# A hybrid decoder layer on one core: doubling steps of a triangular inverse on packed odd rows, and rows of norms by transposes of a repeated column

## The chip, the cores and the metric

The program runs on one core of a Trainium2 chip. The metric is device time in microseconds, as a median of runs. The five engines have a queue each: TensorE (PE in the profile; PEld are its weight loads), VectorE (DVE), ScalarE (ACT), GpSimd (POOL) and SyncE (SP), which issues the DMAs.

## The reference

One decoder layer for a prompt of 2048 tokens (width 1024) and for 8 single-token samples: a mixer, a cross-attention into 256 memory tokens, a SwiGLU, each behind an RMS norm and added to the residual. The mixer's two halves read one input projection: a convolution of width 31, and a gated DeltaNet with 4 heads of 128, whose chunked form solves a unit lower triangular system per chunk and head:

```python
def rms_norm(x, g, eps=1e-6):
    xf = x.astype(jnp.float32)
    y = xf * lax.rsqrt(jnp.mean(xf * xf, axis=-1, keepdims=True) + eps)
    return (y * g.astype(jnp.float32)).astype(x.dtype)
...
    decay = jnp.exp(jnp.where(incl, gc[..., :, None] - gc[..., None, :], -jnp.inf))
    kb = k * beta[..., None]
    lower = jnp.where(strict, jnp.einsum('nbhid,nbhjd->nbhij', kb, k) * decay, 0.0)
    a_mat = lower + jnp.eye(c, dtype=lower.dtype)
    u = lax.linalg.triangular_solve(a_mat, v * beta[..., None], left_side=True, lower=True, unit_diagonal=True)
    w = lax.linalg.triangular_solve(a_mat, kb * jnp.exp(gc)[..., None], left_side=True, lower=True,
                                    unit_diagonal=True)
```

## The kernel before

Activations lie with channels on partitions and tokens along the free axis, in 4 blocks of 512 tokens (b = 0 to 3). The large products split their operands into a high and a low fp32r part and make three passes of them. They run in this order: the input projection for the blocks 0 and 1, then 2 and 3 (tiles hd, glua, glub); the memory's keys and values and the products folded from them (mkv, wk, vp); output projection and attention of the blocks 0 and 1 (rg, sc, rg); then per block the FFN (fx, fy, fz, dn), with output projection and attention of block 2 behind the first FFN and of block 3 behind the second. The first FFN also makes sums of weights that the later ones read back.

Beside these run lanes, Python generators that yield what they wait for. One lane per block and head, `dn_front`, builds the inverse T of the triangular matrix for its 4 chunks of 128 tokens (16 fronts in all); `dn_chain` then runs the recurrence over the chunks. The convolution's taps are 30 VectorE instructions per 128 channels and block (tile cacc).

A front stores lt, the transposed lower matrix, in DRAM and reads its 16x16 diagonal blocks back into 32 partitions, where `base_inverse` inverts them on VectorE (tiles w, x, bit, biq). It writes the inverse blocks to zw and their transposes to zt, both zero elsewhere, and reads W and Tm from there, as 4 chunks of 128x128. Three doubling steps follow, for blocks of s = 16, 32 and 64 (`LEV`). Each makes a product pu1 of lt and Tm, masks and negates it into u1 on VectorE, makes a product pu2 of W and u1, and adds it into Tm's left columns on VectorE; four transposes (ptw) and a ScalarE copy give the next W. The last step only makes the corner block of W, with products of 64 columns. `u1` is one constant tile, 128 x 4 x 128, zeroed at the start. All these products are plain fp32.

A norm's row vector is needed on all partitions. `rstd` gives the reciprocal root r with tokens on partitions (128 x 4, or 128 x 2 for half a block). `spread` turns it: VectorE multiplies the identity by r into dg (128 x 512), TensorE multiplies dg by a matrix of ones (fp32, tile prs), and ScalarE copies the bank to rsb. It runs 13 times: for the input norm of the four blocks, the FFN norm of the four, the final norm of three, and twice, 256 columns each, for the last block's final norm, whose second is on the last stretch of the program.

No instruction goes to an engine as it is written: all are recorded, and `Tape.order` lists them by its own costs and latencies, ready times, free buffers and PSUM banks. Each engine then runs its list in order. There are 8 PSUM banks: 3 "mm" for the large products, 3 "s" for the lanes' steps, one "o" for the chain's output and one "cv" for the convolution; the large products may use the last two only when no chain or no convolution is open. Since every operation is issued by the recorder, all have the line L469 in the profile, and groups are told apart by their tiles; the tiles pu1 and pu2 stand there as pu, and u1 as u. Names of buffers that come from one pool tile (kd, vn, rb and at of a front are halves of tiles named dn) are those of the tile.

Of the kernel before, what the change touches and what calls it, by code (L numbers as in the profile page):

```python
# [14 lines left out]
P = 128  # L15
# [576 lines left out]
def hybrid_step(ctx: ExitStack, tc: tile.TileContext, i: dict, o: list):  # L592
# [486 lines left out]
    def spread(r, n, both=False, spare=RES):  # L1079

        nt = n // P
        yield ("t2", 2 + spare)
        dg = t2("dg", (P, nt, P))
        rb_ = t2("rsb")[:, :n]
        V.tensor_tensor(out=dg, in0=bc(ident, 1, [P, nt, P]), in1=bc(r, 2, [P, nt, P]), op=ALU.mult)
        yield dg
        yield ("ps", "s")
        pb = ps("prs", shape=(P, n))
        mm(pb, ones, dg.rearrange("p t j -> p (t j)"), True, True)
        drop(dg)  # L1090
        A.activation(out=rb_, in_=pb, func=AF.Copy)
        if both:
            return pb, rb_
        yield rb_
        return rb_
# [497 lines left out]

    def base_inverse(x, w, tmp_):
# [4 lines left out]
        for s in (2, 4, 8):  # L1599
# [8 lines left out]
            for step in range(2):  # L1608
# [17 lines left out]
                yield ("dve", 1500)  # L1626

    def dn_front(h, b, sc, prev, out):
# [90 lines left out]
        dma(z_diag(zw[z]), w16[:, 0:256].rearrange("p (j i) -> p j i", i=16))  # L1719
        dma(z_diag(zt_[z]), t16.rearrange("p (j i) -> p j i", i=16))  # L1720
        drop(bit, du)
        W = t2("W", (P, NT, P))
        dma(W, z_full(zw[z]))
# [7 lines left out]
        def left(x, s):  # L1731
            return x.rearrange("p c (b e s) -> p c b e s", e=2, s=s)[:, :, :, 0, :]

        for s in LEV:
            yield ("ps", "s")
            pu = ps("pu1", shape=(P, NT, P))
            for c in range(NT):
                mm(pu[:, c, :], lt[:, c, :], Tm[:, c, :], True, True)
            msk = bc(nms[s].rearrange("p (b s) -> p b s", s=s), 1, [P, NT, 64 // s, s])
            V.tensor_tensor(out=left(u1, s), in0=left(pu, s), in1=msk, op=ALU.mult)  # L1740
            yield u1
            yield ("ps", "s")
            pu = ps("pu2", shape=(P, NT, P))
            if s == LEV[-1]:

                for c in range(NT):
                    mm(pu[0:64, c, 64:P], u1[:, c, 0:64], W[:, c, 64:P], True, True)
                V.tensor_copy(out=W[0:64, :, 64:P], in_=pu[0:64, :, 64:P])
                break
            for c in range(NT):  # L1750
                mm(pu[:, c, :], W[:, c, :], u1[:, c, :], True, True)
            V.tensor_tensor(out=left(Tm, s), in0=left(pu, s), in1=left(Tm, s), op=ALU.add)
            yield Tm
            yield ("ps", "s")
            pt = ps("ptw", shape=(P, NT, P))
            for c in range(NT):
                transpose(pt[:, c, :], Tm[:, c, :], ident)
            drop(W)
            W = t2("W", (P, NT, P))
            A.activation(out=W, in_=pt, func=AF.Copy)  # L1760
            yield W
        drop(lt, Tm)
# [151 lines left out]
    for s in LEV:  # L1914
        m = const(f"nms{s}", [P, 64])
        GS.memset(m, -1.0)
        nb = 64 // s
        GS.affine_select(out=m, in_=m, compare_op=ALU.is_ge, fill=0.0, base=-s, pattern=[[-2 * s, nb], [0, s]], channel_multiplier=1)
        GS.affine_select(out=m, in_=m, compare_op=ALU.is_ge, fill=0.0, base=2 * s - 1, pattern=[[2 * s, nb], [0, s]], channel_multiplier=-1)
        nms[s] = m  # L1920
# [30 lines left out]
    zw = [dram.tile([32, 2064], F32, tag=f"zw{k}", name=f"zw{k}") for k in range(NZ)]  # L1951
# [6 lines left out]
    for k in range(NZ):  # L1958
        for z in (zw[k], zt_[k]):
            dma(z.rearrange("a b -> (a b)").rearrange("(p x) -> p x", p=P), zt)  # L1960
    drop(zt)

    u1s = [const("u1", [P, NT, P])]
    GS.memset(u1s[0], 0.0)
# [879 lines left out]
```

## Time and profile before

| | |
|---|---|
| median of 3 runs | 3009.05 us (3008.03 to 3018.47) |
| the profiled execution | 3007.98 us, span 3006.1 us |
| mean granted TensorE clock | 0.994 |
| busy | PE 2935.5, PEld 2610.7, DVE 2082.1, ACT 1303.0, POOL 1405.4 us |
| instructions of the profile | 53090 |

A matmul of the recorder in fp32 is two MATMUL records in the profile, one in fp32r or a transpose is one. The end of a matmul is modelled, and matmuls overlap their neighbours, so a group's price is better read from starts than from durations. The lists of an engine's instructions, further down, show order alone; they have no times.

### The profile page before, as it was taken

To read this page: it belongs to the slowest core of one execution; us is meant where nothing else is said; L and a number is where in the kernel's file an instruction comes from. 1 tells how busy PE (TensorE), PEld (TensorE's weight loads), DVE (VectorE), ACT (ScalarE), POOL (GpSimd) and SP (SyncE) were. 2 spreads that over 40 slices of the span, in tenths; PEclk is the share of its full clock that TensorE was granted. 3 is DMA by queue.
4 is the path that set the end of the run, shared out by engine and by line. 5 is a ranking of instruction groups with operands and counts; after the bars stand their busy time and mean duration, and the time that the engine had idled before them with its cause. 6 is when DMAs were issued, how large, how long until landed. Compare 5 with 4: busy or idle time off the path is not lost.

```text
span 3006.1 us, 53090 instructions
## 1 busy us (share of the span) xinstructions
PE 2935.5 (98%) x18950; PEld 2610.7 (87%) x18950; DVE 2082.1 (69%) x4280; ACT 1303.0 (43%) x2651; POOL 1405.4 (47%) x1245
## 2 busy tenths in 40 slices
PE   9999999999999999979999999999999999999998
PEld 7899978888888888879988779988888999999997
DVE  8868999988659775987688974543766444664345
ACT  6533455343564434535544453433454233333233
POOL 4434343333645555767886114445413344344444
PEclk9999999999999999999999999999999999999999
DMA  6443334544693433557777657877625666676673
GB/s 218 153 123 95 123 109 135 169 128 131 213 298 106 132 97 93 202 193 265 250 246 268 228 183 238 262 229 228 197 88 170 216 222 216 212 239 218 222 221 129
DMA packets 355175, 560.95 MB, mean 187 GB/s; under 512 B 56448, under 2 KB 154688, under 8 KB 354896
## 3 DMA queue, kind: packets, MB, share of 16 engines
q1 hardware_dynamic: 354912, 557.57, 57.6%
q8 instruction: 150, 2.46, 0.3%
q14 instruction: 113, 0.93, 0.1%
HBM read 449.38 MB, written 108.64 MB: 186 GB/s over the span
## 4 chain that ended last, share of the span: by engine, by line
PE 82%; DVE 10%; DMA 4%; issue 2%; ACT 1%; POOL 1%; SPq 0%; DVEq 0%; POOLq 0%; ACTq 0%
PE dn L469 16%; PE fy L469 12%; PE rg L469 10%; PE hd L469 9%; PE fx L469 8%; PE fz L469 8%; PE sc L469 5%; DVE cacc L469 3%; PE pu L469 2%; PE glua L469 2%; PE glub L469 2%; DVE bit L469 1%; PE pch L469 1%; DVE acc L469 1%; DMA w<-sums 1%
## 5 line engine op out<-in xcount | busy, mean ns | idle before, releaser
L469 POOL TENSOR_TENSOR w<-raw,w 128x512 fp32r<-128x512 f32 x689 | 937.9, 1372 | 965.3 <-ACT w L469 919.0
L469 ACT ACTIVATE w<-raw 128x512 fp32r<-128x512 f32 x912 | 567.7, 630 | 846.7 <-PE fx L469 174.6
L469 PE MATMUL dn<-ff,w 128*128 128x512 f32 (+2 forms) x2688 | 513.5, 347 | 1.2 <-DVE ffs L469 0.5
L469 PEld LDWEIGHTS dn<-ff,w 128*128 128x128 f32 x2688 | 422.8, 188 | 63.2 <-DVE ff L469 1.0
L469 PE MATMUL fy<-op,w 128*128 128x256 f32 (+1 forms) x3168 | 426.2, 282 | 6.9 <-DVE w L469 2.8
L469 PE MATMUL hd<-hT,w 128*128 128x512 f32 (+2 forms) x1920 | 406.7, 360 | 6.2 <-ACT w L469 6.2
L469 PEld LDWEIGHTS fy<-op,w 128*128 128x128 f32 x3168 | 398.7, 189 | 13.7 <-DVE w L469 3.7
L469 DVE SCALAR_TENSOR_TENSOR cacc<-cu,cw,cacc 128x512 f32<-128x512 f32 x480 | 358.0, 746 | 11.5 <-ACT cacc L469 6.9
L469 PEld LDWEIGHTS hd<-hT,w 128*128 128x128 f32 x1920 | 305.6, 191 | 49.6 <-ACT w L469 7.0
L469 DVE TENSOR_TENSOR x<-dn,x 128x512 f32<-128x512 f32 (+1 forms) x448 | 254.0, 571 | 131.1 <-PE dn L469 128.1
L469 PE MATMUL fx<-op,w 128*128 128x256 f32 (+1 forms) x2112 | 285.7, 283 | 11.1 <-ACT ffu L469 11.0
L469 PE MATMUL fz<-op,w 128*128 128x256 f32 (+1 forms) x2112 | 287.7, 283 | 1.8 <-DMA w<-sums 1.7
L469 PEld LDWEIGHTS fx<-op,w 128*128 128x128 f32 x2112 | 269.2, 190 | 18.5 <-ACT ffu L469 11.5
L469 PEld LDWEIGHTS fz<-op,w 128*128 128x128 f32 x2112 | 266.5, 189 | 5.7 <-issue 4.2
L469 DVE TENSOR_TENSOR w<-raw,w 128x512 fp32r<-128x512 f32 x223 | 196.1, 886 | 66.8 <-ACT w L469 66.1
L469 POOL TENSOR_TENSOR sqj<-sqj,sqj 128x512 f32<-128x512 f32 (+1 forms) x98 | 135.0, 1377 | 214.0 <-ACT sqj L469 209.5
L469 DVE TENSOR_TENSOR ffu<-fy,ffu 128x256 f32<-128x256 f32 (+1 forms) x176 | 74.4, 423 | 176.8 <-PE fy L469 176.6
L469 PE MATMUL rg<-catS,w 128*128 128x512 f32 (+1 forms) x960 | 192.1, 354 | 0.8 <-DVE x L469 0.8
L469 PE MATMUL rg<-pT,w 128*128 128x512 f32 x768 | 192.4, 399 | 0.2 <-ACT pT L469 0.2
L469 PE MATMUL sc<-w,hT 128*128 128x512 f32 x768 | 188.5, 399 | 3.3 <-DVE x L469 1.7
L469 PEld LDWEIGHTS rg<-catS,w 128*128 128x128 f32 x960 | 152.0, 188 | 24.2 <-DVE x L469 1.2
L469 PEld LDWEIGHTS sc<-w,hT 128*128 128x128 f32 x768 | 141.2, 188 | 35.9 <-ACT pr L469 3.2
(376 smaller groups left out, 4120.1 us busy)
## 6 DMA issues: line engine op xcount, KB each, us to landing
w<-sums SPq DMA_DIRECT2D x264, 512.0 KB, 4.4
raw<-in_w_gate_dram SPq DMA_DIRECT2D x176, 256.0 KB, 3.1
sums<-w SPq DMA_DIRECT2D x88, 512.0 KB, 3.9
raw<-in_w_down_dram SPq DMA_DIRECT2D x176, 256.0 KB, 3.3
raw<-in_w_up_dram SPq DMA_DIRECT2D x110, 256.0 KB, 3.0
raw<-in_w_in_dram SPq DMA_DIRECT2D x96, 256.0 KB, 2.9
raw<-in_w_out_dram SPq DMA_DIRECT2D x64, 256.0 KB, 4.2
raw<-wk SPq DMA_DIRECT2D x64, 256.0 KB, 3.0
```

What stands on the lines that cost most here:

```text
L469: fn(*args, **kw)
```

## The change

- `spread` no longer makes dg. For each of the 4 (or 2) columns of r, TensorE transposes that column, repeated 128 times by its address pattern, against the identity: 4 (or 2) transposes of 128x128 in place of one fp32 product of 512 (or 256) columns. One less buffer is asked for.
- The doubling steps work on the odd row blocks and left column blocks alone, packed. W for the first step holds the 64 odd rows only (64 x 4 x 128); zw shrinks to 16 x 2080, and its write and read are halved. ScalarE copies the odd columns of lt into lo (128 x 4 x 64). The first pu1 is lo by Tm's left columns (64 weight columns, 64 moving), its pu2 has 64 rows. The middle step keeps 128x128 weights and moves 64 columns in place of 128. The last step takes the columns 64 to 127 of lt and Tm's left 64, leaves its product in the partitions 64 to 127, negates it with a tensor_scalar in place of a mask, and ends with products of 64 rows and 64 columns.
- u1 is 128 x 4 x 64 and is not zeroed any more; there are two masks in place of three.

```diff
     def spread(r, n, both=False, spare=RES):
 
         nt = n // P
-        yield ("t2", 2 + spare)
-        dg = t2("dg", (P, nt, P))
+        yield ("t2", 1 + spare)
         rb_ = t2("rsb")[:, :n]
-        V.tensor_tensor(out=dg, in0=bc(ident, 1, [P, nt, P]), in1=bc(r, 2, [P, nt, P]), op=ALU.mult)
-        yield dg
         yield ("ps", "s")
         pb = ps("prs", shape=(P, n))
-        mm(pb, ones, dg.rearrange("p t j -> p (t j)"), True, True)
-        drop(dg)
+        for t in range(nt):
+            transpose(pb[:, t * P : (t + 1) * P], r[:, t : t + 1].broadcast_to([P, P]), ident)
         A.activation(out=rb_, in_=pb, func=AF.Copy)
...
+    def z_odd(z):
+
+        f = z.rearrange("a b -> (a b)").rearrange("(c x) -> c x", c=NT)
+        return f[:, 0 : 64 * P].rearrange("c (r i) -> r c i", i=P)
+
+    def z_odd_diag(z):
+
+        return z[:, 16 : 16 + 2048].rearrange("p (j i) -> p j i", i=P)[:, :, 0:16]
...
+    def left(x, s, odd=0):
+        return x.rearrange("p c (b e s) -> p c b e s", e=2, s=s)[:, :, :, odd, :]
...
-        dma(z_diag(zw[z]), w16[:, 0:256].rearrange("p (j i) -> p j i", i=16))
+        dma(z_odd_diag(zw[z]), w16[1:32:2, 0:256].rearrange("p (j i) -> p j i", i=16))
         dma(z_diag(zt_[z]), t16.rearrange("p (j i) -> p j i", i=16))
         drop(bit, du)
-        W = t2("W", (P, NT, P))
-        dma(W, z_full(zw[z]))
+        W = t2("W", (64, NT, P))
+        dma(W, z_odd(zw[z]))
         Tm = t2("Tm", (P, NT, P))
         dma(Tm, z_full(zt_[z]))
         yield lambda: prev is None or "done" in prev
...
         u1 = u1s[0]
 
-        def left(x, s):
-            return x.rearrange("p c (b e s) -> p c b e s", e=2, s=s)[:, :, :, 0, :]
-
-        for s in LEV:
+        lo = small("lo", [P, NT, 64], bufs=1)
+        A.activation(out=lo.rearrange("p c (b s) -> p c b s", s=16), in_=left(lt, 16, 1), func=AF.Copy)
+        yield lo
+
+
+        for s in LEV[:-1]:
+            n = nms[s].shape[0]
             yield ("ps", "s")
-            pu = ps("pu1", shape=(P, NT, P))
+            pu = ps("pu1", shape=(n, NT, 64))
             for c in range(NT):
-                mm(pu[:, c, :], lt[:, c, :], Tm[:, c, :], True, True)
-            msk = bc(nms[s].rearrange("p (b s) -> p b s", s=s), 1, [P, NT, 64 // s, s])
-            V.tensor_tensor(out=left(u1, s), in0=left(pu, s), in1=msk, op=ALU.mult)
+                mm(pu[:, c, :], (lo if n == 64 else lt)[:, c, :], left(Tm, s)[:, c], True, True)
+            V.tensor_tensor(out=u1[:n], in0=pu, in1=bc(nms[s], 1, [n, NT, 64]), op=ALU.mult)
             yield u1
             yield ("ps", "s")
-            pu = ps("pu2", shape=(P, NT, P))
-            if s == LEV[-1]:
-
-                for c in range(NT):
-                    mm(pu[0:64, c, 64:P], u1[:, c, 0:64], W[:, c, 64:P], True, True)
-                V.tensor_copy(out=W[0:64, :, 64:P], in_=pu[0:64, :, 64:P])
-                break
+            pu = ps("pu2", shape=(P, NT, 64))
             for c in range(NT):
-                mm(pu[:, c, :], W[:, c, :], u1[:, c, :], True, True)
-            V.tensor_tensor(out=left(Tm, s), in0=left(pu, s), in1=left(Tm, s), op=ALU.add)
+                mm(pu[:, c, :], W[:, c, :], u1[:n, c, :], True, True)
+            V.tensor_tensor(out=left(Tm, s), in0=pu.rearrange("p c (b s) -> p c b s", s=s), in1=left(Tm, s), op=ALU.add)
             yield Tm
...
+        yield ("ps", "s")
+        pu = ps("pu1", shape=(P, NT, 64))
+        for c in range(NT):
+            mm(pu[64:P, c, :], lt[:, c, 64:P], Tm[:, c, 0:64], True, True)
+        V.tensor_scalar(out=u1[64:P], in0=pu[64:P], scalar1=-1.0, scalar2=None, op0=ALU.mult)
+        yield u1
+        yield ("ps", "s")
+        pu = ps("pu2", shape=(64, NT, 64))
+        for c in range(NT):
+            mm(pu[:, c, :], u1[64:P, c, :], W[64:P, c, 64:P], True, True)
+        V.tensor_copy(out=W[0:64, :, 64:P], in_=pu)
+        yield W
         drop(lt, Tm)
...
-    zw = [dram.tile([32, 2064], F32, tag=f"zw{k}", name=f"zw{k}") for k in range(NZ)]
+    zw = [dram.tile([16, 2080], F32, tag=f"zw{k}", name=f"zw{k}") for k in range(NZ)]
...
-    u1s = [const("u1", [P, NT, P])]
-    GS.memset(u1s[0], 0.0)
+    u1s = [const("u1", [P, NT, 64])]
```

Since the order is made from the recorded operations and their costs, it is made anew. Three places follow. A row names the output, the inputs and the shape; a count at its end stands for equal rows.

TensorE, the first front of the program among the products hd of the input projection. Before:

```order
L469 MATMUL pqk_489<-qTd_433,kT_432 128x128 x4
L469 MATMUL hd_483<-hT_237,w_439 128x512 x2
L469 MATMUL pu_291_488<-Tm_470,lt_386 128x128 x4
L469 MATMUL hd_483<-hT_237,w_439 128x512
L469 MATMUL hd_483<-hT_239,w_439 128x512 x3
L469 MATMUL hd_483<-hT_241,w_439 128x512 x3
```

Now:

```order
L469 MATMUL pqk_486<-qTd_430,kT_429 128x128 x4
L469 MATMUL hd_480<-hT_238,w_436 128x512 x3
L469 MATMUL pu_299_495<-Tm_467,lo_485 64x64 x4
L469 MATMUL hd_480<-hT_240,w_436 128x512 x3
L469 MATMUL hd_497<-hT_251,w_434 128x256
L469 MATMUL hd_498<-hT_251,w_434 128x264
```

The group pu1 stands at nearly the same place among the passes of hd, with lo in place of lt and a smaller output.

VectorE, the last rows of the program, the final norm of the last 256 tokens (ms is the mean square, rs its reciprocal root, yl the output). Before:

```order
L469 TENSOR_TENSOR sqj_6077<-sqj_6077,sqj_6095 128x256
L469 TENSOR_SCALAR ms_6097<-pss_6096 128x2
L469 TENSOR_TENSOR dg_6099<-ident,rs_5900_6098 128x256
L469 SCALAR_TENSOR_TENSOR yl_6104<-x_4601,vcol,prs_6103 128x256
L469 SCALAR_TENSOR_TENSOR yl_6104<-x_4602,vcol,prs_6103 128x256
```

Now:

```order
L469 TENSOR_TENSOR sqj_6081<-sqj_6081,sqj_6098 128x256
L469 TENSOR_SCALAR ms_6100<-pss_6099 128x2
L469 SCALAR_TENSOR_TENSOR yl_6104<-x_4608,vcol,prs_6103 128x256
L469 SCALAR_TENSOR_TENSOR yl_6104<-x_4609,vcol,prs_6103 128x256
L469 SCALAR_TENSOR_TENSOR yl_6105<-x_4610,vcol,prs_6103 128x256
```

The row dg is gone; between ms and the first yl VectorE has nothing of its own.

VectorE in the first FFN (ffu, ffs and ff hold a step's gate and product; fx, fy, fz and dn are its PSUM banks; cacc are taps of the last convolution block). Before, inside the sixteenth front's inverse of the 16x16 blocks:

```order
L469 TENSOR_REDUCE w_2698_2896<-bit_2912 32x4x4 x2
L469 TENSOR_TENSOR w_2976<-raw_2948,w_2976 128x512
L469 TENSOR_TENSOR bit_2912<-w_2698_2896,x_2697_2895 32x512
L469 SCALAR_TENSOR_TENSOR cacc_2962<-cu_2938,cw,cacc_2962 128x512
L469 TENSOR_REDUCE biq_2930<-bit_2912 32x64
L469 TENSOR_TENSOR w_2983<-raw_2970,w_2983 128x512
L469 TENSOR_TENSOR bit_2912<-biq_2930,w_2698_2896 32x512
L469 SCALAR_TENSOR_TENSOR cacc_2962<-cu_2938,cw,cacc_2962 128x512
L469 TENSOR_REDUCE w_2698_2896<-bit_2912 32x8x8
L469 TENSOR_TENSOR ff_2936<-ffu_2908,ff_2936 128x512
```

Now, the same inverse of the sixteenth front:

```order
L469 TENSOR_SCALAR w_3055_3252<-x_3054_3251 32x8
L469 TENSOR_TENSOR ff_3259<-ffu_3224,ff_3259 128x512
L469 TENSOR_TENSOR bit_3255<-w_3055_3252,x_3054_3251 32x4x4
L469 TENSOR_TENSOR x_1876<-dn_3269,x_1876 128x512
L469 TENSOR_TENSOR bit_3255<-w_3055_3252,x_3054_3251 32x4x4
L469 TENSOR_REDUCE biq_3271<-bit_3255 32x4 x4
L469 TENSOR_TENSOR bit_3255<-biq_3271,w_3055_3252 32x4x4
L469 TENSOR_TENSOR x_1877<-dn_3270,x_1877 128x512
```

and a stretch earlier in the same FFN, where the taps now stand:

```order
L469 TENSOR_TENSOR ffu_2823<-fz_2825,ffu_2823 128x256
L469 SCALAR_TENSOR_TENSOR cacc_2732<-cu_2722,cw,cacc_2732 128x512
L469 TENSOR_TENSOR w_2833<-raw_2808,w_2833 128x512
L469 TENSOR_TENSOR w_2836<-raw_2769,w_2836 128x512
L469 SCALAR_TENSOR_TENSOR cacc_2732<-cu_2722,cw,cacc_2732 128x512
L469 TENSOR_TENSOR w_2842<-raw_2837,w_2842 128x512
L469 TENSOR_TENSOR dn_2779<-pk_2818,egl_1154 128x512
L469 SCALAR_TENSOR_TENSOR cacc_2732<-cu_2722,cw,cacc_2732 128x512
L469 TENSOR_TENSOR w_2853<-raw_2841,w_2853 128x512
L469 SCALAR_TENSOR_TENSOR cacc_2732<-cu_2722,cw,cacc_2732 128x512
L469 TENSOR_TENSOR w_2854<-raw_2812,w_2854 128x512
L469 SCALAR_TENSOR_TENSOR cacc_2732<-cu_2722,cw,cacc_2732 128x512
```

The sixteenth front's inverse has moved to a later step of that FFN, among rows that read the banks dn and fx to fz, with no taps between; the taps of the last block stand with weight splits (w) instead. The last stretch shown goes on with the product ffu<-ffu,ffs and one more cacc before the next bank is read; dn_2779 in it is a front's kd.

More of the change, by code (lines that the diff above doesn't have):

```diff
@@ L1913, in hybrid_step @@
     nms = {}
-    for s in LEV:
-        m = const(f"nms{s}", [P, 64])
+    for s, n_ in ((16, 64), (32, P)):
+        m = const(f"nms{s}", [n_, 64])
         GS.memset(m, -1.0)
-        nb = 64 // s
-        GS.affine_select(out=m, in_=m, compare_op=ALU.is_ge, fill=0.0, base=-s, pattern=[[-2 * s, nb], [0, s]], channel_multiplier=1)
-        GS.affine_select(out=m, in_=m, compare_op=ALU.is_ge, fill=0.0, base=2 * s - 1, pattern=[[2 * s, nb], [0, s]], channel_multiplier=-1)
+        nb, w_ = 64 // s, n_ // 64 * s
+        GS.affine_select(out=m, in_=m, compare_op=ALU.is_ge, fill=0.0, base=s - w_, pattern=[[-w_, nb], [0, s]], channel_multiplier=1)
+        GS.affine_select(out=m, in_=m, compare_op=ALU.is_ge, fill=0.0, base=w_ - 1, pattern=[[w_, nb], [0, s]], channel_multiplier=-1)
         nms[s] = m
@@ L1958, in hybrid_step @@
     for k in range(NZ):
-        for z in (zw[k], zt_[k]):
-            dma(z.rearrange("a b -> (a b)").rearrange("(p x) -> p x", p=P), zt)
+        dma(zw[k].rearrange("a b -> (a b)").rearrange("(p x) -> p x", p=P), zt[:, 0:260])
+        dma(zt_[k].rearrange("a b -> (a b)").rearrange("(p x) -> p x", p=P), zt)
     drop(zt)
-    u1s = [const("u1", [P, NT, P])]
-    GS.memset(u1s[0], 0.0)
+    u1s = [const("u1", [P, NT, 64])]
     S.add(dec_start())
```

## The prediction

> **What bounds the kernel now.** I read the busy times first, then the slices, then the chain of waits.
>
> ```profile
> span 3006.1 us, 53090 instructions
> PE 2935.5 (98%) x18950; PEld 2610.7 (87%) x18950; DVE 2082.1 (69%) x4280; ACT 1303.0 (43%) x2651; POOL 1405.4 (47%) x1245
> PE   9999999999999999979999999999999999999998
> PE 82%; DVE 10%; DMA 4%; issue 2%; ACT 1%; POOL 1%; SPq 0%; DVEq 0%; POOLq 0%; ACTq 0%
> ```
>
> TensorE is busy almost everywhere, so a microsecond of TensorE work is worth about a microsecond, and work taken from another engine is worth something only where TensorE stands: 3006.1 - 2935.5 = 70.6 us in all. One slice of the forty is below 9. The windows of 75 us and the waits of PE say what is in it:
>
> ```profile
> 1275.00:1350.00 75.00, 59.82 (x392) 53.35 (x391) 65.23 (x126) 27.94 (x49) 53.04 (x41) 0.91 0.58 198
> PE fx L469 <- ACT ffu L469: 11.0, 2, 10.5
> PE pu L469 <- DMA Tm<-zt: 2.9, 2, 2.4
> ```
>
> 15 of the 70.6 us lie there, 10.5 of them in one wait. The doubling steps, on the other hand, are hardly ever waited for: their first groups wait for the DMA of Tm twice, 2.9 us in all. They are filler between groups of the large products, and what counts is the TensorE time that they displace.
>
> **The doubling steps on TensorE.** The view of the tile pu gives each form. An fp32 product is two passes, so a group of four chunks is eight.
>
> ```profile
> L469 PEld LDWEIGHTS pu<-Tm,lt x384: 186/192/193, 138.5 to 1334.7; 128*128 128x128 f32 x192
> L469 PEld LDWEIGHTS pu<-W,u x128: 132/138/139, 167.2 to 1338.9; 128*64 128x64 f32 x128
> ```
>
> The single durations overlap, so I price a group by starts, inside the stream that it interrupts. A pass of 256 columns: 12 fy from 2101.35 to 2102.76 is 0.1175 us; half 256 and half 264 columns, 0.119. Wide (128x128) and transposes:
>
> ```profile
> 142.58 1.05 PE L469 MATMUL pu<-u,W 128*128 128x128 f32 x8
> 143.39 3.12 PE L469 MATMUL hd<-hT,w 128*128 128x256 f32 x24
> 146.34 0.60 PE L469 MATMUL ptw<-ident,Tm 128*128 128x128 f32 x4
> 146.69 1.69 PE L469 MATMUL hd<-hT,w 128*128 128x256 f32 x12
> 148.22 0.60 PE L469 MATMUL pk<-ident,kT 128*128 128x128 f32 x4
> ```
>
> 3.76 us from pu to ptw less 24 x 0.119 leaves 0.90 for eight wide passes (0.112 each); 1.88 less 12 x 0.119 leaves 0.45 for four transposes. Narrow (64 columns of weights, 64 moving columns), and a group with few rows (16 rows by 128 columns of weights, 8 moving):
>
> ```profile
> 289.55 1.69 PE L469 MATMUL hd<-hT,w 128*128 128x256 f32 x12
> 291.16 0.68 PE L469 MATMUL pu<-W,u 128*64 128x64 f32 x8
> 291.77 0.98 PE L469 MATMUL hd<-hT,w 128*128 128x256 f32 x6
> 292.59 0.39 PE L469 MATMUL pch<-S,kT 128*128 128x128 f32 x2
> 292.73 2.39 PE L469 MATMUL hd<-hT,w 128*128 128x256 f32 x18
> ...
> 2101.35 1.57 PE L469 MATMUL fy<-op,w 128*128 128x256 f32 x12
> 2102.76 1.08 PE L469 MATMUL dr<-w,hd_mix 128*16 128x512 f32 x4
> 2103.67 1.11 PE L469 MATMUL fx<-op,w 128*128 128x256 f32 x8
> 2104.71 1.05 PE L469 MATMUL dx<-sel,dr 16*128 16x8 f32 x8
> 2105.70 0.73 PE L469 MATMUL fx<-op,w 128*128 128x256 f32 x4
> 2106.27 0.64 PE L469 MATMUL fz<-op,w 128*128 128x256 f32 x4
> ```
>
> From 289.55 to 292.73 (each the start behind a 128x128 group) 3.18, less 18 x 0.119 and 0.22 for the two pch passes, leaves **0.81** for the narrow group: its passes are half as long, but the stream before and after it loses most of the gain. From 2103.67 to 2106.27, less 12 x 0.1175, the few-row group costs **1.19**, although each of its passes moves only 8 columns. So moving columns do not set these prices at 64 and below 128; weight columns and the switch do.
>
> Before, a front has three wide pu1 groups, two wide pu2 and one narrow: 5 x 0.90 + 0.81 = 5.31 us. After: lo is narrow (0.81); its pu2 has 64 rows and 128 columns of weights, nearest to dx (1.19); the middle step keeps 128 columns of weights and moves 64, still 2 x 0.90; the last two groups are narrow, 2 x 0.81. Sum 5.42: **+0.1 us a front, +1.8 us over 16**. Bounds: if 64 rows cost no more than 128, 0.90 in place of 1.19, -2.9 us; if the last group, with 64 rows too, costs 1.19, +7.9. Two statements of the Trainium skill stand against each other here. "TensorE: Matmul & The Clock Gate" (LDWEIGHTS) says that a load takes its time by columns and the same for 32 rows as for 128: by it the term is -2.9. "TensorEngine Tiling (Array Packing)" (Key Properties) says that a change of tiling mode drains TensorE: that speaks against this change, and the narrow and the few-row rows agree with it.
>
> VectorE gains nothing in these steps (256 elements per partition before and after). ScalarE gets 16 copies lo of 256 elements, about 0.38 us each by the smallest rsb copy (next fence), 6 us on an engine busy 43%. They add a hop ahead of a front's first product; it hides behind the large products, and without that cover, 16 times some 0.5 us, 8 us. The halved zw and W transfers buy nothing: Tm is issued last, unchanged, and is what the first group waited for.
>
> **The norms' rows.**
>
> ```profile
> L469 DVE TENSOR_TENSOR dg<-ident,rs x13: 427/693/1774, 29.4 to 2997.5; 128x512 f32<-128x512 f32 x11, 128x256 f32<-128x256 f32 x2
> L469 ACT ACTIVATE rsb<-prs x13: 383/597/601, 34.0 to 3002.6; 128x512 f32<-128x512 f32 x11, 128x256 f32<-128x256 f32 x2
> 1797.84 1.03 PE L469 MATMUL prs<-dg,ones 128*128 128x512 f32 x2
> 1798.30 1.15 PE L469 MATMUL fz<-op,w 128*128 128x256 f32 x5
> 1799.29 1.59 PE L469 MATMUL fy<-op,w 128*128 128x256 f32 x12
> ```
>
> 1.45 us less 5 x 0.1175 leaves 0.86 for the product of 512 columns; four transposes take 0.45. 11 x 0.41 = 4.5, and 0.2 for the 256-column one inside the last stage: **-4.7 us**. No row shows a repeated column as a TensorE operand: from nothing (transposes at twice the price, 0.90) to these 4.7, I take the whole, since the transposes are otherwise of ptw's form. VectorE loses 13 dg, some 9 us, almost all hidden behind TensorE. The last one is not:
>
> ```profile
> 2996.73 0.71 POOL L469 TENSOR_TENSOR rs<-ms,ex 128x2 f32<-128x2 f32 x1 [1.62 <-DVE ms L469]
> 2997.47 0.43 DVE L469 TENSOR_TENSOR dg<-ident,rs 128x256 f32<-128x256 f32 x1 [0.82 <-POOL rs L469]
> 2998.04 1.19 PE L469 MATMUL prs<-dg,ones 128*128 128x256 f32 x2 [1.59 <-DVE dg L469]
> 2999.28 0.87 DVE L469 SCALAR_TENSOR_TENSOR yl<-x,vcol,prs 128x256 f32<-128x256 f32 x2 [1.38 <-PE prs L469]
> ```
>
> 2.55 us from dg's start to the first yl. Without dg and its hand-over 0.57 goes, and two transposes in place of 1.19 us give some 0.3 more: **-0.9** (bounds 0.5 and 1.3).
>
> **The new order.** Every queue is written anew, so the stall may move. Its place:
>
> ```profile
> 1303.67 0.41 DVE L469 TENSOR_TENSOR ffu<-fy,ffu 128x256 f32<-128x256 f32 x1
> 1316.69 0.67 DVE L469 TENSOR_TENSOR ffu<-ffu,ffs 128x512 f32<-128x512 f32 x1
> 1317.94 0.36 ACT L469 ACTIVATE ffu<-fx 128x256 f32<-128x256 f32 x1
> 1318.50 0.41 DVE L469 TENSOR_TENSOR ffu<-fz,ffu 128x256 f32<-128x256 f32 x1
> L469 DVE SCALAR_TENSOR_TENSOR cacc<-cu,cw,cacc 128x512 f32<-128x512 f32 x480 | 358.0, 746 | 11.5 <-ACT cacc L469 6.9
> L469 DVE TENSOR_TENSOR w<-raw,w 128x512 fp32r<-128x512 f32 x223 | 196.1, 886 | 66.8 <-ACT w L469 66.1
> ```
>
> For 14.8 us VectorE empties no bank of the FFN: the sixteenth front's 16x16 inverses and convolution taps stand there. TensorE runs on for 14.8 - 10.5 = 4.3 us on the banks that it has. In the new order the last inverse stands where no taps are left and banks are emptied in between; the longest stretch without an emptied bank that I find in that stage is six cacc, five w and two products of 512: 6 x 0.746 + 5 x 0.886 + 2 x 0.67 = 10.2 us. 10.2 - 4.3 leaves a stall of some 6 us: **-4**. Bounds: -12 (no stall, and no slow restart: the window's clock was 0.91) and +12 (one more like it).
>
> **Sum.** +1.8 - 4.7 - 0.9 - 4 = -7.8 us on the profiled 3007.98, 3000; its time lies 1.1 under the median 3009.05, so about **3001 us** as the median.
>
> **Rivals.** *Stall gone* (0.20): the new order spreads VectorE's work so that no stall is left in this stage, -3.8 - 12 = -16, 2993. For it: the last inverse and the taps no longer coincide. Against: taps still coincide with the fifteenth. *Narrow is cheap* (0.06): the narrow groups cost only their 0.61 from own start to the next (291.16 to 291.77) and 64 rows cost nothing. The front goes from 5 x 0.90 + 0.61 to 3 x 0.90 + 3 x 0.61, -0.58 x 16 = -9.3, in all -19, 2990. Against: the rows around the groups. The tiling page's "Theoretical Speedup" (TensorEngine Tiling (Array Packing)) promises up to 2x for 64 columns; by that, 0.45 a narrow group, it would be nearer 2985. *A second stall* (0.16, the slower side): the order puts two inverses into the first FFN where one was, and each holds VectorE as at 1303.67. From the point where no bank is emptied for over 4.3 us TensorE stands; one more full stall and the old one kept, -3.8 + 12 to + 16 = 3017 to 3021. *No net change* (0.10): the work saved is lost in small waits, 3009. The forecast has 0.48, with its own range 2994 to 3008.
>
> **How the numbers follow.** The range 2988 to 3015 takes in the stall gone and half of the second stall; what lies outside is the cheap narrow group's lower half and the worst of the slower case. What a measurement of this kernel can tell from no change is about 0.5%, 15 us: faster means below 2994, slower above 3024. Faster: 0.12 of the stall gone, 0.05 of narrow is cheap, 0.10 of the forecast's edge: 0.27. Slower: a part of the second stall, 0.06. The same: 0.67.
>
> **What would show it.** Right: a group pu<-Tm,lo costs about 0.8 us between its neighbours and not 0.45; the 64-row pu<-u,W costs 0.9 to 1.2; prs about 0.45; busy PE falls by 3 us rather than by 15; yl starts 0.9 us sooner after rs; the longest wait of PE in the first FFN is 4 to 8 us. Wrong: PE's busy time down by 10 us or more (then narrow groups are cheap), or more than 80 us of PE idle (then the order decides, and not the work).

## The result, and the profile after

The changed kernel takes **3019.26 us** (median of 20 runs, 3013.06 to 3028.23) against 3011.91 for the kernel before (20 runs). The ratio is **1.0031, 95% interval 1.0023 to 1.0040**: 7 to 12 us slower. The prediction was 3001, with a range of 2988 to 3015. By its own bound of 0.5% this is "the same", which had 0.67; but the sign is wrong, and the time lies outside the range. Three of the 18 us between forecast and result lie in its base, the median of 3 runs, 3009.05; the other 15 are a gain of 8 that was forecast and a loss of 7 that was measured.

The top of the changed kernel's page, and three rows of its waits of PE (total, times, longest, in us):

```profile
span 3019.2 us, 53085 instructions
PE 2941.7 (97%) x18972; PEld 2609.6 (86%) x18972; DVE 2070.6 (69%) x4269; ACT 1301.7 (43%) x2662; POOL 1393.9 (46%) x1239
```

```profile
PE pu L469 <- DMA Tm<-zt: 14.6, 4, 7.7
PE pch L469 <- ACT lny L469: 5.1, 2, 3.5
PE fx L469 <- ACT ffs L469: 3.4, 1, 3.4
```

The span grew by 13.1 us: 6.2 in PE's busy time, which should have fallen by 3, and 6.9 in its idle time (77.5 against 70.6). The two profiled executions lie 4 us under and 2 us over the medians of their kernels, so these 13 us are more than the 7 between the medians, and a few of them are differences between executions.

Most of the rise in busy time is a slower clock. In both traces the granted clock of TensorE falls to 0.50 in stretches of 3.4 us or a multiple of it. Windows laid over these stretches give their length and PE's busy time in them, before and then now:

```profile
sum 38.55, PE 19.51; mean PE 3.25
sum 62.30, PE 41.86; mean PE 4.65
```

At half the clock half of that busy time is lost: 9.8 us before and 20.9 now, by estimate 11 us more. Between the 6.2 measured and the 3 less that were forecast there are 9. So the work came out near its price, and idle time with the slow clock behind it took more than the gain.

The stall of 10.5 us ahead of fx, behind ACT's ffu, is gone. In its place stands a wait that the prediction had set aside, that of a front's first product for the DMA of Tm: 14.6 us where it was 2.9.

The windows cut both kernels at the same three places: the first product fx of the first FFN, the 1008th product rg behind that FFN, and the last dn. The kernel before, then the changed one:

```profile
0.00:1234.00 1234.00, 1204.29 (x7196) 1030.02 (x7197) 1000.57 (x2222) 598.12 (x1288) 556.62 (x619) 1.00 0.47 145
1234.00:1646.00 412.00, 391.81 (x2656) 354.29 (x2655) 332.25 (x511) 200.88 (x394) 319.07 (x229) 0.98 0.71 243
1646.00:2992.00 1346.00, 1337.19 (x9096) 1224.94 (x9094) 742.11 (x1532) 502.90 (x968) 525.85 (x394) 1.00 0.64 208
```

```profile
0.00:1230.50 1230.50, 1191.73 (x7085) 1009.88 (x7085) 989.85 (x2166) 593.99 (x1278) 550.12 (x611) 0.99 0.46 143
1230.50:1657.00 426.50, 407.45 (x2781) 369.55 (x2780) 343.49 (x565) 204.50 (x416) 313.22 (x231) 0.98 0.69 238
1657.00:3006.00 1349.00, 1340.85 (x9105) 1228.98 (x9103) 730.57 (x1525) 502.01 (x965) 526.77 (x394) 0.99 0.62 207
```

Read the first two stages together, for one more front with its chain has slid over the border: 111 passes fewer ahead of it, 125 more behind it. Idle time ahead of the border rose from 29.7 to 38.8 us (1234.00 - 1204.29; 1230.50 - 1191.73), inside the FFN it fell from 20.2 to 19.1. So the new waits lie in the first 1230 us: there three waits for Tm take 6.9 us (one of 2.4 before), two for ACT's lny 5.1 (none before), and the other new ones are of 2.4 us at most. The first FFN exchanged one stall for another: it is 14.5 us longer for 125 passes more, and these are 14 us at 0.112. The last stage took 3 us more although its norms' rows had become cheaper; its clock is 0.99 where it was 1.00.

The longest new wait, in order of time, with VectorE's last step of the inverse, SyncE's queue from the write of zt to the read of Tm, and TensorE:

```profile
1476.97 0.67 DVE L469 TENSOR_REDUCE w<-bit 32x64 f32<-32x512 f32 x1
1478.02 1.69 PE L469 MATMUL fy<-op,w 128*128 128x256 f32 x12 [0.65 <-DVE ffu L469]
1478.98 0.33 SPq L469 DMA_DIRECT2D zt<-x  x1
1479.40 0.44 SPq L469 DMA_DIRECT2D raw<-in_w_gate_dram  x1
1481.91 0.81 SPq L469 DMA_DIRECT2D raw<-in_w_up_dram  x2
1482.84 0.38 SPq L469 DMA_DIRECT2D Tm<-zt  x1
1487.43 1.09 PE L469 MATMUL pu<-Tm,lo 128*64 128x64 f32 x8 [7.71 <-DMA Tm<-zt]
```

From the end of the inverse (1477.64) to the product it is 9.8 us: a copy, a write to memory (1478.98), the read of it (1482.84), and its landing. Between write and read SyncE's list holds three loads of weights, and for the second of them SyncE stood 2.0 us, until GpSimd had done with its buffer; what part of these 3.9 us the landing of the write would have taken anyway the trace does not show. TensorE's list reaches pu at 1479.7, 2 us after the inverse. In the kernel before, the sixteenth front's first product waited 0.56 us.

### The profile page after: what moved, and what is told of

Its sections match the earlier page's. It is cut to its first block, busy times and chain, and to the rows that moved or that the text cites. A ratio compares the mean times of both kernels' runs of the same rounds, so it can differ in the third digit from the quotient of the medians.

```text
span 3019.2 us, 53085 instructions
## 1 busy us (share of the span) xinstructions
PE 2941.7 (97%) x18972; PEld 2609.6 (86%) x18972; DVE 2070.6 (69%) x4269; ACT 1301.7 (43%) x2662; POOL 1393.9 (46%) x1239
## 4 chain that ended last, share of the span: by engine, by line
PE 61%; DVE 5%; DMA 4%; POOL 2%; issue 1%; ACT 1%; SPq 0%; POOLq 0%; DVEq 0%; ACTq 0%
PE dn L469 14%; PE fy L469 11%; PE rg L469 10%; PE fx L469 8%; PE fz L469 8%; PE sc L469 5%; PE pu L469 1%; DVE cacc L469 1%; DVE w L469 1%; POOL w L469 1%; DVE x L469 1%; PE mkv L469 1%; PE podd L469 1%; PE pch L469 0%; PE dr L469 0%
## 5 line engine op out<-in xcount | busy, mean ns | idle before, releaser
L469 PE MATMUL hd<-hT,w 128*128 128x512 f32 (+2 forms) x1920 | 400.6, 358 | 7.4 <-ACT w L469 5.7
L469 PE MATMUL rg<-catS,w 128*128 128x512 f32 (+2 forms) x960 | 187.7, 352 | 1.5 <-ACT jn L469 1.4
L469 PEld LDWEIGHTS rg<-pT,w 128*128 128x128 f32 x768 | 141.7, 189 | 34.7 <-DVE pT L469 2.3
```

The costliest lines, as they stand in the source:

```text
L469: fn(*args, **kw)
```

## The experiments

The order of TensorE's work is the order in which the planner records it; the other engines' lists are sorted by the planner's second clock. Both use the planner's prices. So every edit that alters a price writes a new order for all engines. Nothing below leaves out any of the computation. The last column counts the fronts, of sixteen, whose doubling steps TensorE meets only after the first fx of the first FFN.

| kernel | this, us | before, us | ratio, 95% interval | fronts in the FFN |
|---|---|---|---|---|
| the change | 3019.26 | 3011.91 | 1.0031 (1.0023 to 1.0040) | 2 |
| norms' rows alone | 3013.41 | 3012.95 | 0.9996 (0.9984 to 1.0008) | 2 |
| doubling steps alone | 3047.40 | 3012.95 | 1.0105 (1.0087 to 1.0123) | 3 |
| change, Tm counted 6 us later | 3085.40 | 3012.95 | 1.0235 (1.0215 to 1.0255) | 3 |
| before, Tm counted 6 us later | 3042.24 | 3012.95 | 1.0083 (1.0063 to 1.0102) | 3 |
| doubling steps, PE in before's order | 3016.67 | 3011.07 | 1.0013 (1.0000 to 1.0027) | 1 |
| norms' rows, PE in before's order | 3019.90 | 3011.07 | 1.0025 (1.0013 to 1.0038) | 1 |
| both, PE in before's order | 3015.58 | 3011.07 | 1.0010 (0.9998 to 1.0021) | 1 |
| both, first step with 128 rows, PE in before's order | 3017.63 | 3011.07 | 1.0017 (1.0004 to 1.0029) | 1 |
| norms' rows, all engines in before's order | **3002.52** | 3011.93 | **0.9966 (0.9956 to 0.9977)** | 1 |
| both, 128 rows, all engines | 3005.35 | 3011.93 | 0.9979 (0.9968 to 0.9989) | 1 |
| before, counted at the new steps' price | 3071.69 | 3011.93 | 1.0196 (1.0179 to 1.0213) | 3 |
| before, a transpose counted at 112 ns | 3038.29 | 3011.93 | 1.0085 (1.0067 to 1.0103) | 2 |
| the change, all engines in before's order | **3007.97** | 3014.22 | **0.9980 (0.9970 to 0.9990)** | 1 |
| change, transpose at 112 ns | 3042.98 | 3014.22 | 1.0092 (1.0076 to 1.0109) | 2 |
| change, transpose at 108 ns | 3041.39 | 3014.22 | 1.0089 (1.0074 to 1.0105) | 3 |
| before, transpose at 108 ns | 3031.32 | 3014.22 | 1.0051 (1.0034 to 1.0068) | 2 |
| before, transpose at 104 ns | 3015.26 | 3011.96 | 1.0013 (1.0003 to 1.0022) | 1 |
| change, new steps at their measured price | 3035.73 | 3011.96 | 1.0084 (1.0066 to 1.0102) | 2 |

### One part of the change at a time

The functions `spread` or the doubling steps are taken from the kernel before, the rest from the change.

> The norms' rows alone, on the kernel before; the doubling steps are the old ones. Theory A (the work is priced rightly, and the +7 us of the whole change is stalls of TensorE that the new order of the instructions brings, with the slow clock behind them): the work is 5.6 us less, so 3006 us, plus or minus some 8 us that the order gives or takes; whatever departs from 3006 stands in the idle time of PE and in windows with a granted clock below 1. Theory B (the new doubling groups cost some 15 us more than their prices, in what they do to the stream around them): 3006, with PE busy down by about 5 and idle as before. Theory C (the transposes of a repeated column cost more than the 0.45 us a group): slower than 3012, with PE busy not below 2935.

> The doubling steps alone, with the old product for the norms' rows. Theory A: work +2.5 us, so 3014 us, plus or minus some 8 of order; the idle time of PE and the waits for Tm tell which. Theory B: 3012 + 15 = 3027, with the waits for Tm as few as before (under 4 us) and the time in PE busy. Theory C: 3012 + 2.5 = 3014, and no more.

The norms' rows gave nothing (3013.4) and the doubling steps cost 34 us, yet both together cost 7. Parts that do not add up do not measure work alone. Theory B has more than its size here, but not its marks: the run's waits for Tm were 10.6 us and not below 4, and idle time rose by 17 us beside 19 of busy time. Theory C stays possible.

### Later products for the fronts

```diff
         dma(Tm, z_full(zt_[z]))
+        C.ready[Tm.name] += 6000.0
```

> The changed kernel with the same work, where the planner's clock takes Tm for ready 6 us later, so that a front's first product stands some 6 us later in TensorE's order. Theory A: the waits of PE for the DMA of Tm fall from 14.6 us to under 4, the time falls by 8 to 14 us, to 3005 to 3011, unless the moved groups meet another stall (which would then be a wait of more than 4 us for something else). Theory B: the groups are the same, so 3019 plus or minus 3.

> The kernel before with the same clock correction and the same work. It has 2.9 us of waits for Tm to lose. Theory A (order decides, several us either way, for equal work): anywhere from 3000 to 3022, more than 4 us from 3012 as likely as not, with the difference in idle time and slow clock and the work of PE unchanged. Theory B (order is worth little, prices decide): 3009 to 3013.

The remedy that Theory A gave made things worse, by the ratios by 61 and by 25 us. The waits for Tm rose to 25.5 us in the changed kernel and to 4.6 in the old one, so most of the old one's loss lies elsewhere. What hangs on a front moves later with it; which part of that costs the time is not shown. Both results lie outside A's ranges (3005 to 3011, 3000 to 3022). What stands of it is that order moves equal work: 25 us between two orders of the old work, where B allowed 2.

### The same order on TensorE

The planner is told the old price for the new work: each group of the doubling steps, the transfers of zw and W, the copy lo at nothing; and the four transposes at the price of the product with dg's time still counted.

```diff
-                mm(pu[:, c, :], W[:, c, :], u1[:n, c, :], True, True)
+                mm(pu[:, c, :], W[:, c, :], u1[:n, c, :], True, True, cost=(216.33, 235.99) if s == 16 else (216.33, 235.99))
...
-            transpose(pb[:, t * P : (t + 1) * P], r[:, t : t + 1].broadcast_to([P, P]), ident)
+            transpose(pb[:, t * P : (t + 1) * P], r[:, t : t + 1].broadcast_to([P, P]), ident, (3 + n * 4 / 2.4) / nt)
```

> The new doubling steps alone, but the planner counts each of their groups, transfers and copies at the price of the old one, so that TensorE's order is word for word that of the kernel before (the other engines' differ in under 4% of their instructions); the copy lo is one more on ScalarE. Theory D (the work is worth its prices, and the planner's own prices, which take a product by its moving columns and so count a front of the new steps at 2.6 us where it takes 5.4, write the order that loses the time): work +2.5 us on 3013, so 3015, within 4 us, against 3047 for the same work in the order that the planner writes by itself. Theory B (the groups disturb the stream beyond their prices): 3025 or more, with PE busy up by over 12 us.

> The norms' rows by transposes alone, with the four transposes counted at the price of the product that they replace, and the product dg still counted on VectorE though it isn't there: TensorE's order is that of the kernel before, with prs in its place. Theory D: work -5.6 us, so 3007, within 4 us, where the planner's own order gave 3013. Theory C (the transposes are not worth it at all): 3013 again.

> Both parts of the change in the order of the kernel before, by the same two corrections. Theory D: +2.5 - 5.6 = -3.1 us, so 3010, within 4 us, where the change itself took 3019; the stall of 10.5 us before fx near 1308 us is still there, and the waits for the DMA of Tm are back under 5 us. Theory B: 3020 or more.

> Both parts in the order of the kernel before, and the first doubling step with all 128 rows, moving only the even blocks (W and its transfer are the old, whole ones, and the copy lo is gone): a front is 4 x 0.89 + 2 x 0.80 = 5.17 us in place of 5.27 before and 5.42 in the change. Theory D: -0.1 x 16 - 5.6 = -7.2 us, so 3006, within 4 us: under both kernels. Theory B: the 64-row groups were what disturbs, so 3006 here too, but 3020 or more in the run with them.

The doubling steps settle Theory B: with TensorE's order held, they cost 0.13%, 4 us, and not 34. Its page, beside PE's 2935.5 and a span of 3006.1 before:

```profile
span 3008.6 us, 53101 instructions
PE 2936.6 (98%) x18950; PEld 2599.5 (86%) x18950; DVE 2079.3 (69%) x4280; ACT 1307.7 (43%) x2665; POOL 1406.8 (47%) x1242
```

The other three missed. The norms' rows took 3020 where 3007 was due. TensorE's order was that of the kernel before, but with dg gone a quarter of VectorE's list had moved (1034 rows of 4282; in the doubling steps' run under 4%). Idle time rose by 8.7 us, to 79.3, with no new wait longer than 5 us, and PE's busy time by 4 where it should have fallen by 5. Either the transposes are not worth their price, or VectorE's order counts as much as TensorE's.

### The same order on every engine

dg stays in the planner as an operation that is laid out and never issued.

```diff
-        V.tensor_tensor(out=dg, in0=bc(ident, 1, [P, nt, P]), in1=bc(r, 2, [P, nt, P]), op=ALU.mult)
+        Engine(Ghost(tape, "dve"), "dve", C).tensor_tensor(out=dg, in0=bc(ident, 1, [P, nt, P]), in1=bc(r, 2, [P, nt, P]), op=ALU.mult)
```

> The norms' rows by transposes, with every engine in the order of the kernel before: the planner still lays out the product dg as if it were there, and only its issue is left out (15 rows of VectorE's list differ, 2 of SP's). In the run that held TensorE's order alone, a quarter of VectorE's list (1034 rows of 4282) had moved, and it took 3020. Theory E (the order of VectorE and the transfers decides as much as that of TensorE; the transposes are worth their price): 3012 - 5.6 = 3006 us, within 4 us, and PE busy 5 us down with the idle time at 70 to 74. Theory C (the transposes are worth nothing, or their saving returns as waits in any order): 3011 or more.

> Both ideas in the order of the kernel before on every engine: the norms' rows as in the run beside it, and the doubling steps that move the even blocks alone, with all 128 rows and without the copy lo (counted by the planner as the old ones; 150 rows of VectorE's list differ). Theory E: work -5.6 - 1.6 = -7.2 us, so 3005, within 4 us, under both kernels. Theory C: 3012 or more.

> Both parts of the change as they are (64-row groups, copy lo), with every engine in the order of the kernel before: dg planned but not issued, the doubling steps counted as the old ones. Theory E: the parts add: -9 (the norms' rows in that order) + 4 (the doubling steps in it), so 3007 us, within 4, where the change in its own order takes 3019; the 12 us between are then the order alone. Otherwise (the parts disturb each other in any order): 3015 or more.

Theory E holds. The norms' rows by transposes, in the old order:

```profile
span 3000.9 us, 53120 instructions
PE 2931.0 (98%) x18972; PEld 2611.9 (87%) x18972; DVE 2069.7 (69%) x4267; ACT 1302.1 (43%) x2651; POOL 1407.2 (47%) x1245
```

PE's busy time is 4.5 us down and idle time 69.9, as it was; the spans of the two profiled executions are 5.2 apart, for a price of 5.6. All runs taken, the gain is 0.34%, 7 to 13 us, which is more than the price; no run shows where the rest comes from. This kernel beats both. The whole change in the old order is 0.20% *faster* than the kernel before, 3 to 9 us, where its price says 3. It is the sum of its parts: 0.9966 x 1.0013 = 0.9979, the second with TensorE's order alone held. The step with 128 rows, priced 4 us under the change's, came out at 0.9979 too; that difference is not resolved.

So the work was worth a small gain, and the change's own order costs 1.0031 - 0.9980 = 0.51%, 15 us, against the old order.

### What a new order is worth

First the wrong price: the planner's recording clock takes a product by its moving columns and counts a front's new steps at 2.6 us, the old ones at 4.8.

> The kernel before, all its work unchanged; only the planner counts the groups of the doubling steps at the price that it gives to the changed ones (2.6 us a front in place of 4.8; the chip takes 5.3). Theory D (the wrong price writes an order that loses time, whatever the work): 3030 to 3050, as the doubling steps alone in their own order, 3047. Theory F (any new order loses some 5 to 10 us against this one, and the price of the groups has no part in it): 3015 to 3025. Theory B (order is worth little, the new groups cost the time): 3012.

Unchanged work, and 60 us lost, more than any of the three theories allowed. Its waits, its stage of the first FFN, and TensorE there:

```profile
PE pu L469 <- DMA Tm<-zt: 26.9, 3, 15.9
```

```profile
1204.00:1706.00 502.00, 445.41 (x2924) 400.95 (x2923) 397.76 (x685) 223.31 (x466) 315.32 (x240) 0.92 0.62 211
```

```profile
1459.71 1.57 PE L469 MATMUL fy<-op,w 128*128 128x256 f32 x12
1477.21 2.04 PE L469 MATMUL pu<-Tm,lt 128*128 128x128 f32 x8 [15.92 <-DMA Tm<-zt]
1479.77 2.08 PE L469 MATMUL pu<-u,W 128*128 128x128 f32 x8 [0.52 <-DVE u L469]
1482.36 1.11 PE L469 MATMUL ptw<-ident,Tm 128*128 128x128 f32 x4 [0.52 <-DVE Tm L469]
```

268 passes more than before stand in this stage, 30 us of work at 0.112, and it is 90 us longer. A front's steps follow one another here with no large product between them: each hop to VectorE shows as a wait of half a microsecond, and each group takes 2.0 us where it takes 1.0 at the full clock; the granted clock is 0.50 there. Of the 60 us beyond the work some 36 are idle time and 24 busy time, with a mean clock of 0.92 in the stage where it was 0.98.

Then orders with no meaning, and the true prices:

```diff
-        C.run("pe", 110.0, [in_], out, 90.0)
+        C.run("pe", 112.0, [in_], out, 90.0)
```

> The kernel before, all its work unchanged; the planner counts a transpose at 112 ns in place of 110, a change with no meaning, and writes another order from about 300 us on. It measures what a new order alone is worth. Theory F (the order of before is a good draw among many): 3015 to 3045. Theory G (orders for the right work are all alike within a few us, and only a wrong price hurts): 3008 to 3016.

> The kernel before, its work unchanged, a transpose counted at 108 ns: a second draw for the old work beside 3038. Theory F (before stands on a good draw): 3020 to 3045. Theory G: 3008 to 3016.

> The changed kernel with all its work, its planner counting a transpose at 112 ns in place of 110. Theory F (a new order for this work is a draw, and the change's own, 3019, was a good one): 3025 to 3060. Theory G' (the change's own order is a bad draw, and most others are better): 3005 to 3018.

> The same with 108 ns: a second draw for the changed work. Theory F: 3025 to 3060. Theory G': 3005 to 3018.

By the ratios, two nanoseconds in one price cost the old work 26 and 15 us, and the changed work 18 and 17 us beyond the change's own order. Theory F is right: before stands on a good draw, and the change's own order is a good one for its work as well, only not so good. Theory D, that the wrong price is to blame, fails in the last test:

> The changed kernel with all its work; its planner counts the groups of the doubling steps as the trace measured them, 0.80, 1.23, 0.89, 0.89, 0.81 and 0.80 us, 5.4 a front in place of 2.6. Two fronts stand in the first FFN, as in the change's own order. Theory D (the wrong price is what loses the time): 3005 to 3015. Theory H (the count of fronts): 3013 to 3043, as the other orders with two.

With the measured prices the planner writes an order of 3036 us.

The tile ptw shows how many fronts are late: two groups of four for each front. Three kernels from their first fx on: before, the change, before at the new price.

```profile
L469 PE MATMUL ptw<-ident,Tm x8: 270/272/273, 1327.8 to 1333.2; 128*128 128x128 f32 x8
```

```profile
L469 PE MATMUL ptw<-ident,Tm x16: 270/273/421, 1351.5 to 1498.9; 128*128 128x128 f32 x16
```

```profile
L469 PE MATMUL ptw<-ident,Tm x24: 271/421/476, 1327.3 to 1560.2; 128*128 128x128 f32 x24
```

One front: 3002 to 3020 us. Two: 3013 to 3043. Three: 3041 to 3085. This was read off the other kernels of the table, except the last, before it was tested in one more:

> The kernel before, its work unchanged, the planner counting a transpose at 104 ns in place of 110. In the orders run so far the time goes with the number of the sixteen fronts whose doubling steps TensorE meets only in the first FFN stage: one front, 3002 to 3020 us; two, 3013 to 3043; three, 3041 to 3085. Of nine such prices this is the only one besides 110 that leaves one front there. Theory H (that count decides): 3005 to 3018. Theory F (any new order is a loss against the order of before, whatever the count): 3025 to 3045.

At 104 ns one front is left there, and the time is 3015, as Theory H said. The count is a good sign, shown once by forecast. It is not the whole cause: the change's own two fronts cost no idle time inside the FFN, the rise stands ahead of it, and the norms' rows with VectorE's list moved lost 8 us against before, 18 against the same work with every list held, with a single front. The ranges of one and of two fronts overlap, too. Which of many small waits makes one order better than another stays open.

## Why the prediction was wrong, point by point

**The bound.** Right as far as shown. "A microsecond of TensorE work is worth about a microsecond" held where every engine's order was held: the whole change gained 3 to 9 us for a price of 3, the norms' rows 7 to 13 for 5.6, and with TensorE's order alone held the doubling steps cost 0 to 8 for 2.

**The doubling steps on TensorE: +0.1 us a front, +1.8.** Right. The changed kernel's fifteenth front, whole groups with the stream around them:

```profile
1342.69 1.32 PE L469 MATMUL dn<-ff,w 128*128 128x512 f32 x5
1343.94 0.68 PE L469 MATMUL pu<-Tm,lo 128*64 128x64 f32 x8
1344.55 1.70 PE L469 MATMUL fy<-op,w 128*128 128x256 f32 x12
1346.08 1.54 PE L469 MATMUL dn<-ff,w 128*128 128x512 f32 x6
1347.55 1.10 PE L469 MATMUL pu<-u,W 64*128 64x64 f32 x8
1348.59 3.04 PE L469 MATMUL dn<-ff,w 128*128 128x512 f32 x12
1351.46 0.60 PE L469 MATMUL ptw<-ident,Tm 128*128 128x128 f32 x4
1351.82 3.70 PE L469 MATMUL dn<-ff,w 128*128 128x512 f32 x15
1355.35 1.00 PE L469 MATMUL pu<-Tm,lt 128*128 128x64 f32 x8
...
1369.01 1.58 PE L469 MATMUL fy<-op,w 128*128 128x256 f32 x12
1370.43 0.86 PE L469 MATMUL fz<-op,w 128*128 128x256 f32 x6
1371.22 0.67 PE L469 MATMUL pu<-W,u 64*64 64x64 f32 x8
1371.83 0.98 PE L469 MATMUL fz<-op,w 128*128 128x256 f32 x6
1372.64 1.59 PE L469 MATMUL fy<-op,w 128*128 128x256 f32 x12
```

A pass of 512 columns is 0.235 us (15 dn, 1351.82 to 1355.35). From 1342.69 to 1346.08, less 5 x 0.235 and 12 x 0.1175, lo costs 0.80 (predicted 0.81). From 1346.08 to 1351.46, less 18 x 0.235, the 64-row group costs 1.15 (1.19; the runs above reckon with 1.23). From 1369.01 to 1372.64, less 24 x 0.1175, the last group, 64 rows by 64 columns, costs 0.81 (0.81): the upper bound of 7.9 us is out, and so is *narrow is cheap*. With the middle groups at 0.91 a front takes 5.4 us, as predicted, and the run in the old order put the whole term at +4 (0 to 8), the copy lo included. The Trainium skill, "TensorE: Matmul & The Clock Gate" (LDWEIGHTS), says that the number of rows does not matter to a load; the prediction took from it 0.90 for the 64-row group and -2.9 for the term. The trace agrees on the loads, but not on the group. The loads of that group, and loads and products of the next pu2, with 128 rows:

```profile
1347.55 0.96 PEld L469 LDWEIGHTS pu<-u,W 64*128 64x128 f32 x8 [0.36 <-DVE ffu L469]
1358.96 0.97 PEld L469 LDWEIGHTS pu<-u,W 128*128 128x128 f32 x8
1359.07 1.00 PE L469 MATMUL pu<-u,W 128*128 128x64 f32 x8
```

Eight loads take as long with 64 rows as with 128. The group still costs 1.15 against 0.91. With 128 rows the first load starts 0.11 us ahead of the first product (1358.96, 1359.07), under the product before; with 64 rows both start at 1347.55, after 0.36 us without a load. So a part of the price stands where the form changes, and not in the length of a load.

**The norms' rows: -4.7 us, and -0.9 in the tail.** Right.

```profile
2315.24 0.60 PE L469 MATMUL prs<-ident,rs 128*128 128x128 f32 x4
2315.60 1.69 PE L469 MATMUL fx<-op,w 128*128 128x260 f32 x12
2317.12 1.13 PE L469 MATMUL fz<-op,w 128*128 128x260 f32 x8
```

1.88 us less 12 x 0.119 leaves 0.45 for four transposes of a repeated column, as for four plain ones: the repeat costs nothing. The tail:

```profile
3010.74 0.71 POOL L469 TENSOR_TENSOR rs<-ms,ex 128x2 f32<-128x2 f32 x1 [1.62 <-DVE ms L469]
3011.51 0.69 PE L469 MATMUL prs<-ident,rs 128*128 128x128 f32 x2 [1.04 <-POOL rs L469]
3012.23 3.22 DVE L469 SCALAR_TENSOR_TENSOR yl<-x,vcol,prs 128x256 f32<-128x256 f32 x8 [1.57 <-PE prs L469]
```

From rs to yl 1.49 us, where it was 2.55: 1.06 sooner. (The prediction called the 2.55 "from dg's start"; it was counted from the start of rs.)

**The new order: -4, from -12 to +12.** This step failed. Its size was 15 us of loss, by the two runs of the whole change, and it was reasoned from one stall only. That stall did go; the waits that came were elsewhere, 9 us of idle time ahead of the first FFN, and the clock of 0.50 behind waits took by estimate 11 us of busy time more. What the step took for granted is that the rest of the order stays as good as it was; nine orders that were not written to mend anything or to make it worse (the own orders of the change and of its two parts, five by a transpose at 104 to 112 ns, one by the measured prices) lie 4 to 34 us above the same work in the old order (of TensorE alone for the doubling steps; by the ratios: 0.13% for before at 104 ns, 1.12% for the change at 112), and none below it. "The doubling steps are hardly ever waited for" was true of that order alone.

**The rivals.** *A second stall* (0.16) named the time, 3017 to 3021, and the two fronts in the first FFN, but not the way: idle time there did not grow, its longest wait is 7.7 us and is for Tm, not for an emptied bank. *Stall gone* came true without its gain. *No net change* (0.10) had the mechanism nearest to what the runs show, the work saved and lost again in waits, but priced it to come out even, at 3009. The sign "longest wait 4 to 8 us" was met for the wrong reason, and "busy PE falls by 3 us" failed: it rose by 6.2. The sign that the order decides, more than 80 us of PE idle, was not met either (77.5), although the order decided: the prediction looked for that loss in idle time alone, and the larger part of it stood in busy time, at the slow clock.

## What to carry to other kernels

Price the work and the order apart: to measure a small edit in a kernel whose order a planner writes, hold the old order by counting new work at the old price, on every engine and not on the busiest alone. Where a tuned order is written anew, expect a loss of the size that a meaningless edit gives, and measure that size first; here it was 4, 15 and 26 us on the old work, where the work at stake was 3. A small gain is then kept by fixing the order, as the norms' rows were.

## What was not expected of the hardware

A wait costs more than itself. In the kernel before, the stream behind the stall of 10.5 us:

```profile
1318.36 2.93 PE L469 MATMUL fx<-op,w 128*128 128x256 f32 x12 [10.51 <-ACT ffu L469]
1321.09 1.66 PE L469 MATMUL fz<-op,w 128*128 128x256 f32 x8
```

Twelve passes of 256 columns take 2.73 us there, against 1.41 at the full clock: half speed. The granted clock (in the row, ahead of the last two figures) says for how long:

```profile
1308.66:1322.31 13.65, 3.95 (x18) 0.50 0.63 198
```

It is 0.50 for 4 us of work behind the wait. The Trainium skill, "TensorE: Matmul & The Clock Gate" (What's actually happening), describes this gate, half the clock after an idle window and the full clock after about 3.4 us of work. The trace agrees on the way back, and not quite on the way down: the clock fell 0.8 us into the wait, after 3.4 us in which TensorE was busy for 1.43, and at 724.98 us it fell with no wait over 1.3 us in the 3.4 us before.

So busy time can rise with idle time when the work is the same. Before with a transpose at 112 ns has 14.6 us more idle and 14.1 us more busy; 40.80 us of its busy time lie at the clock of 0.50, where it was 19.51, and half of the difference is 10.6, by estimate most of the 14.1. Before at the new price has 33.4 us more idle and 28.7 more busy. At 108 ns it was 10.0 and 3.7, with a mean clock as high as before: the second part of the cost does not follow every wait.
